# Splits of the second query slab's rotated halves put off by eight steps, first two rounds of attention spread wider

## The chip, the cores and the metric

The kernel runs on one core of a Trainium2 chip, as one program in one launch. The metric is the time of one execution in microseconds (us), as the device gives it. A profiled execution of the kernel before belongs to the numbers; where an engine's busy time, a wait or a line is named, it is from that one execution.

The engines are TensorE (PE in the profile, with PEld for its weight loads), VectorE (DVE), ScalarE (ACT), GpSimd (POOL) and SyncE (SP), whose queue here issues nearly all DMAs.

## What is computed

Two decoder layers over x of 512 x 1024 float32. Cut to what matters:

```python
def hybrid_layer(x, w_in, w_out, g_pre, g_post, lb, g_head, sinks):
    h = rms_norm(x, g_pre)
    q_h, f_h, i_h, z_h, q_a, k_a, v_a, z_a = split(h @ w_in)      # 1024 -> 6400 columns
    o_h = rms_norm(hgrn2(q_h, f_h, i_h, lb), g_head) * silu(z_h)  # 8 heads of 128, gated recurrence
    q_a, k_a = rotary(q_a, pos), rotary(k_a, pos)                 # 16 query heads, 2 key heads of 64
    o_a = sliding_window_attention(q_a, k_a, v_a, sinks) * silu(z_a)   # window 128, blocks of 128
    return x + rms_norm(concat([o_h, o_a]) @ w_out, g_post)
```

The attention takes, for each block of 128 queries, the scores against its own and the previous block of keys, masks them to the window, takes a softmax with one sink term per head, and sums the values.

## The kernel before

**Projections.** The weights come from HBM in pieces of 128 x 512 float32 and are split on the chip into a high half (`whi`, a cast on ScalarE, L176) and a low half (`wlo`, a subtraction on VectorE, L177); activations are split in the same way. A product of two such numbers takes three matmuls, so each step of a projection issues three matmuls of 128 x 512 into a `pj` buffer of PSUM (L282). A unit is eight steps (24 matmuls) that add into one buffer; two units run interleaved. `step()` issues one step, counts down the list `waiting`, and starts the weight conversions that are due at that step count. `later(steps, key, fn)` puts a function on that list: it runs when so many steps have been issued.

**Weight buffers.** Four `raw` buffers take the DMAs on SyncE's queue; nine `whi` and nine `wlo` buffers hold the halves. SyncE issues in order, so a weight load that waits for a free `raw` buffer holds up what stands behind it.

**Queries.** The query projection comes in two slabs of weights (QA and QA + 1) of four units each. Two units make one group g of four heads, so the first slab gives g = 0 and 1, the second g = 2 and 3. `evac` of `qa_stream` is called at the end of each unit. After the first unit of a group it multiplies by cosine and sine on VectorE (L493, L494); after the second it does the same (L499, L500), adds and subtracts on GpSimd (L503, L504), splits the two rotated halves (two casts on ScalarE, L506, and two subtractions on VectorE, L507) and stores them to HBM in two DMAs (L509). `load_q(g)` reads them back in four DMAs in the layout that attention needs (L483).

**Attention.** `att_stream` runs 16 rounds (g, n), g from 0 to 3 and block n from 0 to 3. Round i issues the scores of round i (L531 for n = 0, otherwise two halves, L542), the transposes of the probabilities of round i - 2 (L569) and the value product of round i - 4 (L595). A round's softmax goes through several engines: VectorE masks the scores (L534 or L546), takes the row maxima (L535 or L547) and from them `negm` (L550) and `ds` (L552); ScalarE takes four exponentials out of the score buffer (L556) and that of the sink (L559); VectorE adds and inverts the sums (L560, L561); GpSimd normalises (L563). After the transposes ScalarE and VectorE split the result (L328, L329) and GpSimd masks it twice (L581). Scores and transposes share three PSUM buffers (`sc_78`, `sc_79`, `sc_80`) in turn. The queries of groups 2 and 3 are loaded after rounds 3 and 7, into the two buffers of groups 0 and 1, and first needed in rounds 8 and 12.

**What sets the order.** The attention's rounds and the projections are merged by shares: each stream has a total, and the stream whose share done is the smallest goes next.

```python
def merge(*streams):
    live = [[g, 0.0, float(total)] for g, total in streams]
    while live:
        s = min(live, key=lambda e: e[1] / e[2])
        try:
            s[1] += next(s[0]) or 1.0
```

Each function of a round yields 1 / (functions in that round), so a round counts 1 in a total of 20 (16 rounds and `VLAG` = 4). The program so written is then put in order engine by engine by a scheduler, which moves an instruction ahead of others of its engine if it sees it ready earlier. `pin(ins)` fixes an instruction behind the one written before it on the same engine; the attention's matmuls are pinned, the projection's are not.

Of the kernel before, what the change touches and what calls it, by code (L numbers as in the profile page):

```python
# [11 lines left out]
F32R = mybir.dt.float32r  # L12
U8 = mybir.dt.uint8
AF = mybir.ActivationFunctionType
ALU = mybir.AluOpType
# [5 lines left out]
NT = SEQ // 128  # L21
# [8 lines left out]
QA, IV, FQ, ZA, ZH = 0, 2, 4, 8, 10  # L30
# [4 lines left out]
HG_N = 28.5  # L35
VLAG = 4
QWAIT = 8
DEFER = 18
PJ, SC = 3, 3
LEAD, SPACE = 20, 3  # L40
# [6 lines left out]
# [6 lines that stand above are left out]
        except StopIteration:  # L53
            live.remove(s)
# [13 lines left out]
def hybrid_kernel(ctx: ExitStack, tc: tile.TileContext, x, wkv, win, wout, g_pre, g_post, lbp, ghead, sinks,  # L68
                  gcol_c, cos_f, sin_f, cos_t, sin_t, masks_c, out):
    nc = tc.nc  # L70
# [55 lines left out]
    for l in range(1, DEPTH):  # L126
        i = plan_order.index((l, "kv"))
# [69 lines left out]
    def later(steps, key, fn):  # L197

        waiting.append([steps, key, fn])
# [6 lines left out]
    def ensure(key):  # L206
        while key not in emitted:
            run_first()
# [92 lines left out]
    def through(key):  # L301
        while slab_done[key] < slab_steps[key]:
            step()
            yield 1.0

    def until(cond):
        while not cond():
            step()
# [10 lines left out]
    def proj_feat(key, l, evac):  # L319

        enqueue(key, [(range(KT), lambda k, w, m=m: tuple(t[:, k % 4 * P:(k % 4 + 1) * P] for t in w[2 * m + k // 4]),
                       lambda k, w: (hT[l][0][:, k, :], hT[l][1][:, k, :]), lambda o, m=m: evac(m, o),
                       [("h", l, tt) for tt in range(NT)]) for m in range(4)])
# [33 lines left out]
    class Norm:  # L357
# [47 lines left out]
        def rest(self, c):  # L405
            self.turn(c)
            self.high(c)
            self.low(c)
            if self.tt == NT - 1 and c == 1:
                state["limit"] = None  # L410
# [15 lines left out]
    def layer(l, last):  # L426
# [51 lines left out]
        qs, stacks = {}, {}  # L478

        def load_q(g):  # L480
            st = big.tile([P, 4, 512], F32R, tag="b8", name="qs", bufs=2)
            for row, j, i in ((0, 1, 0), (32, 0, 1), (64, 0, 0), (96, 1, 1)):
                nc.sync.dma_start(st[row:row + 32].bitcast(F32), stacks[g][j, i].rearrange("(h p) t -> p h t", h=4))  # L483
            qs[g] = st

        def qa_stream(s):
            hold = {}

            def evac(m, o):
                cosf, sinf = rot[0][:, 0], rot[0][:, 1]  # L490
                if m % 2 == 0:
                    hold["a"] = a = big.tile([P, 2, 512], F32, tag="oy", name="rot", bufs=6)
                    nc.vector.tensor_tensor(a[:, 0], o, cosf, op=ALU.mult)  # L493
                    nc.vector.tensor_tensor(a[:, 1], o, sinf, op=ALU.mult)  # L494
                    return
                g = 2 * s + m // 2
                a = hold["a"]
                b = big.tile([P, 2, 512], F32, tag="oy", name="rot", bufs=6)
                nc.vector.tensor_tensor(b[:, 0], o, sinf, op=ALU.mult)  # L499
                nc.vector.tensor_tensor(b[:, 1], o, cosf, op=ALU.mult)  # L500
                stack = dr.tile([2, 2, P, 512], F32, tag="stack", name="stack", bufs=4)

                nc.gpsimd.tensor_tensor(a[:, 0], a[:, 0], b[:, 0], op=ALU.subtract)  # L503
                nc.gpsimd.tensor_tensor(b[:, 1], b[:, 1], a[:, 1], op=ALU.add)  # L504
                for r, h in ((a[:, 0], b[:, 0]), (b[:, 1], a[:, 1])):
                    nc.scalar.copy(h.bitcast(F32R), r)  # L506
                    nc.vector.tensor_tensor(r.bitcast(F32R), r, h, op=ALU.subtract)  # L507
                for j, t in ((0, a), (1, b)):
                    nc.sync.dma_start(stack[j].rearrange("i p t -> p i t"), t)  # L509
                stacks[g] = stack  # L510
                if g < 2:
                    load_q(g)

            proj_feat(("in", l, QA + s), l, evac)

# [72 lines left out]
        def att_value(g, n, terms):  # L588
            v = g // 2
            t_ = slice(n * P, (n + 1) * P)  # L590
            if g == len(oa):
                oa.append(big.tile([P, 2, 512], F32, tag="oy", name="oa", bufs=6))
            U = ac()
            for i, (blk, d) in enumerate(terms):
                pin(nc.tensor.matmul(U, lhsT=vst[v][:, blk, :], rhs=d, start=(i == 0), stop=(i == len(terms) - 1)))  # L595
            ul = tmp("u")
            nc.scalar.copy(ul[0:64, :], U[64:128, :])
            Uv = U.rearrange("p (a b t) -> p a b t", a=2, b=2)
            lv = ul.rearrange("p (a b t) -> p a b t", a=2, b=2)
            for b in range(2):  # L600
                nc.vector.tensor_tensor(oa[g][64 * b:64 * b + 64, :, t_], Uv[0:64, :, b, :], lv[0:64, :, b, :], op=ALU.add)

        def att_stream(steps):


            pts, terms = {}, {}
            n = len(steps)
            for tt in range(NT):
                ensure(("k", l, tt))
            for i in range(n + VLAG):  # L610
                todo = []
                if i < n:
                    todo.append(lambda: pts.update({i: att_scores(*steps[i])}))
                if 2 <= i <= n + 1:
                    todo.append(lambda: terms.update({i - 2: att_transpose(*steps[i - 2], pts.pop(i - 2), i % 2)}))
                if i >= VLAG:
                    todo.append(lambda: att_value(*steps[i - VLAG], terms.pop(i - VLAG)))
                for fn in todo:
                    fn()
                    yield 1.0 / len(todo)  # L620

                if i < n and steps[i][1] == NT - 1 and steps[i][0] < 2:
                    until(lambda: steps[i][0] + 2 in stacks)
                    load_q(steps[i][0] + 2)
# [235 lines left out]
        def final(tt, ch, c0, n):  # L860
# [38 lines left out]
            if not last:  # L899
                pre_norm(tt, xt, hT2["gpre"], hT[l + 1], ("h", l + 1, tt), DEFER)  # L900

# [11 lines left out]
        def run():  # L913
            hg = lambda a: (hgrn(a), HG_N)
            rest = lambda key: (through(key), remaining(key))
            until(lambda: 1 in qs)
            for _ in range(QWAIT):
                step()
            merge((att_stream([(g, n) for g in range(4) for n in range(NT)]), 4 * NT + VLAG), rest(("in", l, FQ)))
            merge(hg(0), rest(("in", l, FQ + 1)))  # L920
            merge(hg(2), rest(("in", l, FQ + 2)))
            merge(hg(4), rest(("out", l, "a1")))
            merge(hg(6), rest(("out", l, "h0")))
            kv_room.add(l + 1)
            drain(through(("out", l, "h1")))
# [47 lines left out]
    m, n = head[0], head[1]  # L973
# [146 lines left out]
```

## Time and profile before

| | us |
|---|---|
| median of 3 runs | 934.13 (933.86 to 934.25) |
| the profiled execution | 933.88 |
| its span, first to last instruction | 932.1 |
| around the span | 1.78 |

A profile row of an instruction has its start in us from the start of the span, its duration in us, engine, line, operation, output <- inputs and the count of instructions merged in it; in brackets stands how long its engine was idle before it and whose end released it. Durations of instructions that follow each other on an engine overlap by some hundredths. The granted clock is the share of TensorE's full clock that the throttle let through. The scores of the first attention round start at 58.96 us in layer 0 and at 517.94 us in layer 1.

### The profile page before, as it was taken

What the parts mean: (1) busy time and instruction counts of PE and PEld (TensorE: products, weight loads), DVE (VectorE), ACT (ScalarE), POOL (GpSimd) and SP (SyncE); (2) the same over time, 40 slices, a digit from 0 to 9 for tenths busy, and PEclk for the clock granted to TensorE, in tenths of its full rate; (3) what the DMA queues carried; (4) which work ended last, traced back from release to release, by engine and by line L of the source; (5) the groups of instructions that cost most, each with busy time, mean ns of one, the idle gap of its engine ahead of it and who ended that gap; (6) DMA issues with size and microseconds to landing.
All of it is one profiled execution on the core that took longest, in us unless ns stands there. A gap on an engine that the chain in (4) does not pass through costs nothing.

```text
span 932.1 us, 18970 instructions
## 1 busy us (share of the span) xinstructions
PE 910.0 (98%) x7240; PEld 753.3 (81%) x7240; DVE 670.9 (72%) x1326; ACT 462.8 (50%) x1100; POOL 271.5 (29%) x286
## 2 busy tenths in 40 slices
PE   8998999999999999999989989999999999999996
PEld 7886888878788788788878868888787887887885
DVE  5978777885766783955786788677877577749556
ACT  5535658636464451444453456684554736325242
POOL 3435444232221311311232345441323212113102
PEclk9999999999999999999999989999999999999998
DMA  7685413322222142424356554123223223323313
GB/s 221 193 226 156 124 39 101 91 82 80 68 85 96 62 141 64 138 69 123 111 162 179 171 159 136 35 82 101 70 79 89 71 80 105 111 69 93 91 34 135
DMA packets 56570, 100.74 MB, mean 108 GB/s; under 512 B 6560, under 2 KB 9120, under 8 KB 56480
## 3 DMA queue, kind: packets, MB, share of 16 engines
q1 hardware_dynamic: 56192, 99.40, 35.7%
q8 instruction: 57, 0.93, 0.4%
q14 instruction: 33, 0.27, 0.1%
q10 hardware_dynamic: 288, 0.14, 0.1%
HBM read 86.93 MB, written 12.58 MB: 107 GB/s over the span
## 4 chain that ended last, share of the span: by engine, by line
PE 86%; DVE 6%; ACT 3%; POOL 2%; issue 2%; DMA 1%; SPq 0%; POOLq 0%; DVEq 0%; ACTq 0%
PE pj L282 71%; PE ac L595 2%; PE sc L703 2%; PE sc L542 2%; PE ac L772 2%; ACT s L556 1%; PE ac L775 1%; PE ac L760 1%; PE sc L569 1%; DVE wlo L177 1%; PE sc L820 1%; POOL r L343 1%; PE sc L750 1%; PE sc L714 1%; DVE a L896 1%
## 5 line engine op out<-in xcount | busy, mean ns | idle before, releaser
L282 PE MATMUL pj<-hhi,wlo 128*128 128x512 f32 x512 | 205.8, 402 | 0.0
L177 DVE TENSOR_TENSOR wlo<-raw,whi 128x512 fp32r<-128x512 f32 x249 | 182.9, 748 | 30.0 <-ACT whi L176 28.5
L282 PE MATMUL pj<-hhi,whi 128*128 128x512 f32 x512 | 200.0, 391 | 0.0
L282 PE MATMUL pj<-hlo,whi 128*128 128x512 f32 x512 | 199.5, 390 | 0.0
L176 ACT CAST whi<-raw 128x512 fp32r<-128x512 f32 x256 | 154.5, 621 | 87.9 <-PE pj L282 74.7
L282 PE MATMUL pj<-whi,ops 128*128 128x512 f32 (+1 forms) x520 | 173.5, 395 | 0.0
L282 PEld LDWEIGHTS pj<-whi,ops 128*128 128x128 f32 x520 | 97.2, 188 | 19.6
L282 PEld LDWEIGHTS pj<-hhi,whi 128*128 128x128 f32 x512 | 96.1, 188 | 20.9
L282 PEld LDWEIGHTS pj<-hhi,wlo 128*128 128x128 f32 x512 | 96.2, 188 | 18.7
L282 PEld LDWEIGHTS pj<-hlo,whi 128*128 128x128 f32 x512 | 96.3, 188 | 18.0
L282 PE MATMUL pj<-whi,hlo 128*128 128x512 f32 x256 | 104.5, 408 | 0.7 <-ACT whi L176 0.7
L282 PE MATMUL pj<-wlo,hhi 128*128 128x512 f32 x256 | 101.0, 395 | 2.0 <-DVE wlo L177 2.0
L282 PE MATMUL pj<-whi,hhi 128*128 128x512 f32 x256 | 101.0, 394 | 0.0
L282 PE MATMUL pj<-wlo,ops 128*128 128x512 f32 (+1 forms) x260 | 100.5, 386 | 0.0
L721 POOL TENSOR_TENSOR k<-k,tot 128x256 f32<-128x256 f32 x80 | 64.2, 822 | 109.4 <-PE sc L703 60.7
L556 ACT ACTIVATE s<-sc,negm 128x128 f32<-128x128 f32 x128 | 45.4, 368 | 36.8 <-DVE negm L550 26.1
L720 DVE TENSOR_TENSOR q<-q,tot 128x256 f32<-128x256 f32 x80 | 50.6, 665 | 14.6 <-PE sc L703 9.4
L282 PEld LDWEIGHTS pj<-wlo,hhi 128*128 128x128 f32 x256 | 48.8, 191 | 10.7 <-DVE wlo L177 2.3
L282 PEld LDWEIGHTS pj<-whi,hhi 128*128 128x128 f32 x256 | 48.6, 190 | 10.6
L282 PEld LDWEIGHTS pj<-whi,hlo 128*128 128x128 f32 x256 | 48.6, 190 | 9.6 <-ACT whi L176 1.1
L282 PEld LDWEIGHTS pj<-wlo,ops 128*128 128x128 f32 x260 | 49.0, 188 | 8.7
L563 POOL TENSOR_TENSOR s<-s,sums 128x512 f32<-128x512 f32 x32 | 35.8, 1119 | 57.0 <-ACT a L328 28.4
(185 smaller groups left out, 1418.7 us busy)
## 6 DMA issues: line engine op xcount, KB each, us to landing
raw<-in_win_dram SPq DMA_DIRECT2D x192, 256.0 KB, 2.7
raw<-in_wout_dram SPq DMA_DIRECT2D x64, 256.0 KB, 2.7
stack<-rot SPq DMA_DIRECT2D x16, 512.0 KB, 3.6
qs<-stack SPq DMA_DIRECT2D x32, 256.0 KB, 4.9
a<-in_x_dram SPq DMA_DIRECT2D x12, 256.0 KB, 3.1
raw<-in_wkv_dram SPq DMA_DIRECT2D x8, 256.0 KB, 3.7
x_mid<-a SPq DMA_DIRECT2D x8, 256.0 KB, 2.3
a<-x_mid SPq DMA_DIRECT2D x8, 256.0 KB, 3.0
```

The lines of the kernel that those rows point to most:

```text
L176: keep(nc.scalar.copy(hi, v))
L177: keep((nc.gpsimd if i in on_pool and i % 2 else nc.vector).tensor_tensor(lo, v, hi.bitcast(F32), op=ALU.subtract))
L282: nc.tensor.matmul(u.o, lhsT=u.sta(k, u.w)[i], rhs=u.mov(k, u.w)[j], start=(n == 0), stop=(n == len(u.list) - 1))
L343: keep(nc.gpsimd.tensor_tensor(r, t, mhalf[:, 0:1], op=ALU.pow))
L542: pin(nc.tensor.matmul(S[:, h * 256:(h + 1) * 256], lhsT=q[:, 2 * hp_ + h, t_], rhs=kst[v][p][:, (n - 1) * P:(n + 1) * P], start=(h == 0 a ...
L556: nc.scalar.activation(pt[:, h * P:(h + 1) * P], cur[h], AF.Exp, bias=negm[:, h:h + 1], scale=SCALE, accum_out=sums[:, h:h + 1])
L563: nc.gpsimd.tensor_tensor(pv, pv, sums.unsqueeze(2).broadcast_to([P, 4, P]), op=ALU.mult)
L595: pin(nc.tensor.matmul(U, lhsT=vst[v][:, blk, :], rhs=d, start=(i == 0), stop=(i == len(terms) - 1)))
L703: pin(nc.tensor.matmul(L[32 * b:32 * b + 32, c:c + 16], lhsT=k[:, o_:o_ + 32], rhs=qv[:, blk:blk + qu, 1, :], start=True, stop=True, tile_ ...
L720: nc.vector.tensor_tensor(qv[:, :, 1, :], qv[:, :, 1, :], tv[:, :, 0].unsqueeze(2).broadcast_to([P, nb, hh]), op=ALU.mult)
L721: nc.gpsimd.tensor_tensor(kv_[:, :, 0, :], kv_[:, :, 0, :], tv[:, :, 1].unsqueeze(2).broadcast_to([P, nb, hh]), op=ALU.mult)
L772: pin(nc.tensor.matmul(O[:, c], lhsT=A[:, c], rhs=vs(j, n), start=(n == 0), stop=False))
```

## The change

It has two parts.

The splits of the rotated halves, the stores and the entry in `stacks` move into a function `rest`. For groups 0 and 1 it is called at once, as before. For groups 2 and 3 it goes to `later(ROT_WAIT, ...)`, so it is written out eight projection steps (24 matmuls) later, and its two casts are pinned, behind whatever was last written for ScalarE then. The multiplications and GpSimd's sums stay where they were.

The first two rounds of attention yield 1.75 in place of 1 each, and the total of the stream grows by 1.5: more projection steps are placed in these rounds, and fewer in the later ones.

```diff
+ROT_WAIT = 8
+SLOW = (2, 1.75)
...
-                for r, h in ((a[:, 0], b[:, 0]), (b[:, 1], a[:, 1])):
-                    nc.scalar.copy(h.bitcast(F32R), r)
-                    nc.vector.tensor_tensor(r.bitcast(F32R), r, h, op=ALU.subtract)
-                for j, t in ((0, a), (1, b)):
-                    nc.sync.dma_start(stack[j].rearrange("i p t -> p i t"), t)
-                stacks[g] = stack
+
+                def rest():
+                    for r, h in ((a[:, 0], b[:, 0]), (b[:, 1], a[:, 1])):
+                        keep = pin if g >= 2 else lambda ins: ins
+                        keep(nc.scalar.copy(h.bitcast(F32R), r))
+                        nc.vector.tensor_tensor(r.bitcast(F32R), r, h, op=ALU.subtract)
+                    for j, t in ((0, a), (1, b)):
+                        nc.sync.dma_start(stack[j].rearrange("i p t -> p i t"), t)
+                    stacks[g] = stack
+                    if g < 2:
+                        load_q(g)
+
                 if g < 2:
-                    load_q(g)
+                    rest()
+                else:
+                    later(ROT_WAIT, None, rest)
...
                 for fn in todo:
                     fn()
-                    yield 1.0 / len(todo)
+                    yield (SLOW[1] if i < SLOW[0] else 1.0) / len(todo)
...
-            merge((att_stream([(g, n) for g in range(4) for n in range(NT)]), 4 * NT + VLAG), rest(("in", l, FQ)))
+            merge((att_stream([(g, n) for g in range(4) for n in range(NT)]), 4 * NT + VLAG + SLOW[0] * (SLOW[1] - 1)), rest(("in", l, FQ)))
```

The lines below the change are numbered higher by 2 to 10 in the kernel after: the casts L506 are L511 there, the subtractions L507 are L512, L176 and L177 are L178 and L179, L531 and L542 are L541 and L552, L546 and L547 are L556 and L557, L550 is L560, L556 is L566.

How far the projection has come when the scores of a round are issued, in projection matmuls since the scores of round 0, counted in TensorE's order (where the two halves stand apart, the first):

| round | 1 | 2 | 3 | 4 | 5 | 8 | 12 | 15 |
|---|---|---|---|---|---|---|---|---|
| layer 0, before | 0 | 18 | 36 | 56 | 72 | 123 | 195 | 246 |
| layer 0, now | 12 | 42 | 57 | 84 | 90 | 145 | 204 | 252 |
| layer 1, before | 0 | 20 | 40 | 55 | 67 | 121 | 190 | 241 |
| layer 1, now | 7 | 37 | 52 | 72 | 85 | 140 | 199 | 247 |

TensorE, layer 1, from the scores of round 0 (L531) to those of round 1 (L542), before:

```order
L531 MATMUL sc_80<-kst,qs 128x128 x8
L542 MATMUL sc_78<-kst,qs 128x256 x4
L542 MATMUL sc_79<-kst,qs 128x256 x4
L282 MATMUL pj<-hhi,whi 128x512
L282 MATMUL pj<-hhi,wlo 128x512
```

And now:

```order
L541 MATMUL sc_80<-kst,qs 128x128 x8
L284 MATMUL pj<-hhi,whi 128x512
L284 MATMUL pj<-hhi,wlo 128x512
L284 MATMUL pj<-hlo,whi 128x512
L284 MATMUL pj<-hhi,whi 128x512
L284 MATMUL pj<-hhi,wlo 128x512
L284 MATMUL pj<-hlo,whi 128x512
L284 MATMUL pj<-hhi,whi 128x512
L552 MATMUL sc_78<-kst,qs 128x256 x4
L552 MATMUL sc_79<-kst,qs 128x256 x4
```

Seven projection matmuls have come between the two rounds.

ScalarE, layer 1, around the casts of group 3 before (`rot`; `whi` are weights, `a<-sc` the split of the transposes, `u` a value product):

```order
L559 ACTIVATE es<-ds 128x4
L506 CAST rot<-rot 128x512
L176 CAST whi<-raw 128x512 x2
L506 CAST rot<-rot 128x512
L176 CAST whi<-raw 128x512 x2
L328 CAST a<-sc_78 128x512
L597 COPY u<-ac 64x512
```

The same stretch of ScalarE's queue now, where the casts are those of group 2 and the exponentials (L566) those of round 3:

```order
L330 CAST a<-sc_79 128x512
L178 CAST whi<-raw 128x512
L566 ACTIVATE s,sums<-sc_80,negm 128x128
L178 CAST whi<-raw 128x512
L566 ACTIVATE s,sums<-sc_80,negm 128x128
L178 CAST whi<-raw 128x512
L511 CAST rot<-rot 128x512 x2
L178 CAST whi<-raw 128x512
L566 ACTIVATE s,sums<-sc_78,negm 128x128 x2
L569 ACTIVATE es<-ds 128x4
```

The casts of group 3 no longer stand in front of these weight casts; they come three rounds later. Those of group 2, which stood before the exponentials of round 2, have taken a place behind three weight casts and among the exponentials of round 3.

VectorE, layer 0, around the subtractions of group 3 before (`wlo` are weight low halves, `mx` row maxima, `oa` the attention's output):

```order
L499 TENSOR_TENSOR rot<-pj,cs 128x512
L500 TENSOR_TENSOR rot<-pj,cs 128x512
L177 TENSOR_TENSOR wlo<-raw,whi 128x512
L534 COPY_PREDICATED sc_80<-masks,neg 128x512
L177 TENSOR_TENSOR wlo<-raw,whi 128x512
L507 TENSOR_TENSOR rot<-rot 128x512
L177 TENSOR_TENSOR wlo<-raw,whi 128x512 x2
L507 TENSOR_TENSOR rot<-rot 128x512
L535 TENSOR_REDUCE mx<-sc_80 128x4
L329 TENSOR_TENSOR a<-sc_78,a 128x512
L550 SCALAR_TENSOR_TENSOR negm<-mx,nsnk 128x4
```

And now, with the subtractions of group 2, in round 3:

```order
L556 COPY_PREDICATED sc_80<-masks,sc_80 128x2x128
L556 COPY_PREDICATED sc_78<-masks,sc_78 128x2x128
L557 TENSOR_REDUCE mx<-sc_80 128x2
L179 TENSOR_TENSOR wlo<-raw,whi 128x512
L557 TENSOR_REDUCE mx<-sc_78 128x2
L179 TENSOR_TENSOR wlo<-raw,whi 128x512 x2
L512 TENSOR_TENSOR rot<-rot 128x512 x2
L179 TENSOR_TENSOR wlo<-raw,whi 128x512
L560 SCALAR_TENSOR_TENSOR negm<-mx,nsnk 128x4
L331 TENSOR_TENSOR a<-sc_79,a 128x512
```

Before, two subtractions and four weight low halves stood around the masking and in front of the maxima of round 4; now the same number stands between the maxima of round 3 and its `negm`.

## The prediction

> **What bounds the kernel now.** I read the page first, then the busy time by stretches, then TensorE's instructions in order of time, then the chain of waits and the other engines where TensorE stood. A round is one step of `att_stream`: S(i) are its score matmuls, T(i) its transposes. The three score buffers go round, so S(i+1) and T reuse what the exponentials of earlier rounds must first have read.
>
> ```profile
> span 932.1 us, 18970 instructions
> PE 910.0 (98%) x7240; PEld 753.3 (81%) x7240; DVE 670.9 (72%) x1326; ACT 462.8 (50%) x1100; POOL 271.5 (29%) x286
> PEclk9999999999999999999999989999999999999998
> ```
>
> TensorE is the bound: 910.0 of 932.1 us. Nothing is to be won but where it stands or runs slowly. The change touches the attention rounds alone, 60 to 160 us in layer 0 and 520 to 620 in layer 1. Busy time by stretches (from:to, length; busy time of PE, PEld, DVE, ACT and POOL, each with its instructions; granted clock; DMA share; GB/s):
>
> ```profile
> 60.00:100.00 40.00, 35.98 (x189) 29.61 (x189) 34.99 (x79) 21.60 (x82) 20.07 (x17) 1.00 0.56 151
> 100.00:160.00 60.00, 59.70 (x313) 50.12 (x313) 46.17 (x114) 39.64 (x126) 27.94 (x25) 1.00 0.34 93
> 520.00:580.00 60.00, 55.93 (x275) 45.60 (x274) 52.22 (x113) 36.04 (x125) 28.80 (x25) 0.94 0.50 143
> 540.00:545.00 5.00, 3.12 (x7) 2.51 (x8) 5.00 (x8) 2.73 (x5) 1.28 (x1) 0.62 0.34 116
> 545.00:550.00 5.00, 5.00 (x21) 4.20 (x20) 3.67 (x10) 2.47 (x11) 3.17 (x3) 0.70 1.03 390
> ```
>
> TensorE is idle for 4.02 us (40.00 - 35.98) and 0.30 us in layer 0 and for 4.07 us in layer 1. In layer 1 its clock also falls, to 0.62 and 0.70: 3.12 x 0.38 + 5.00 x 0.30 = 2.69 us. In all 11.08 us can be won. TensorE's longest waits, with what ended them:
>
> ```profile
> 66.31 0.74 PE L542 MATMUL sc<-kst,qs 128*128 128x256 f32 x4 [0.77 <-ACT s L556]
> 72.24 1.44 PE L542 MATMUL sc<-kst,qs 128*128 128x256 f32 x8 [0.61 <-ACT s L556]
> 87.72 0.52 PE L569 MATMUL sc<-ident,s 128*128 128x128 f32 x3 [1.64 <-DVE negm L550]
> 89.24 0.74 PE L542 MATMUL sc<-kst,qs 128*128 128x256 f32 x4 [1.00 <-ACT s L556]
> 539.40 0.50 PE L282 MATMUL pj<-whi,hlo 128*128 128x512 f32 x1 [0.71 <-ACT whi L176]
> 541.88 0.80 PE L282 MATMUL pj<-wlo,hhi 128*128 128x512 f32 x1 [1.99 <-DVE wlo L177]
> 554.30 0.74 PE L542 MATMUL sc<-kst,qs 128*128 128x256 f32 x4 [0.37 <-ACT s L556]
> 579.13 1.44 PE L542 MATMUL sc<-kst,qs 128*128 128x256 f32 x8 [0.23 <-ACT s L556]
> ```
>
> They are of two kinds. At 66.31 and 72.24 the scores of rounds 2 and 3 come before the exponentials of the round before have read the buffer: the rounds stand too close. The larger ones come from the rotated halves of the fourth query group. In layer 0 ScalarE stands 3.94 us at their cast (first row), and the `negm` of the row maxima, queued on VectorE behind the subtractions that wait for the casts, ends only at 87.64:
>
> ```profile
> 82.21 0.62 ACT L506 CAST rot<-rot 128x512 fp32r<-128x512 f32 x1 [3.94 <-POOL rot L503]
> ```
>
> ```profile
> 82.86 1.56 DVE L507 TENSOR_TENSOR rot<-rot 128x512 fp32r<-128x512 f32 x1
> ...
> 85.69 0.68 DVE L507 TENSOR_TENSOR rot<-rot 128x512 fp32r<-128x512 f32 x1
> 86.30 0.68 DVE L535 TENSOR_REDUCE mx<-sc 128x4 f32<-128x512 f32 x1
> 86.90 0.68 DVE L329 TENSOR_TENSOR a<-sc,a 128x512 fp32r<-128x512 f32 x1
> 87.49 0.15 DVE L550 SCALAR_TENSOR_TENSOR negm<-mx,nsnk 128x4 f32<-128x4 f32 x1
> ```
>
> In layer 1 the chain of waits shows the same: GpSimd's rotation, then the cast, then the subtraction. Behind these two stand the weight casts and low halves of which the projection waits for one, the 0.71 and 1.99 above.
>
> ```profile
> 536.89 1.29 POOL rot L503
> 538.18 0.02 issue
> 538.21 0.63 ACT rot L506
> 538.83 0.02 issue
> 538.86 0.04 DVE rot L507
> ```
>
> **The change part by part.** Wider spacing. Before, no projection matmul stands between S(0) and S(1), and 18 (layer 0) or 20 to 24 (layer 1) between S(1) and S(2); now 12 or 7, and then 30. The time of matmuls as they go by without waits, from the chain of waits:
>
> ```profile
> 99.99 0.48 PE sc L542 x4
> 100.47 1.39 PE pj L282 x6
> 101.86 0.43 PE sc L569 x4
> ```
>
> One projection matmul is 1.39 / 6 = 0.23 us, half the scores of a round 0.48 and the transposes 0.43, and 30 matmuls 6.9 us. What they must cover, by durations of single rows:
>
> ```profile
> 62.66 0.75 DVE L547 TENSOR_REDUCE mx<-sc 128x2 f32<-128x256 f32 x2
> 67.78 0.75 DVE L546 COPY_PREDICATED sc<-masks,sc 128x256 f32<-128x256 uint8 x2
> L552 DVE TENSOR_TENSOR ds<-snk,negm x32: 148/162/1253, 62.6 to 615.6; 128x4 f32<-128x4 f32 x32
> 87.68 1.52 ACT s L556 x8
> ```
>
> Masking 0.75, maxima 0.75, `negm` 0.15 and all four exponentials 1.52 make 3.2 us. One of the small steps can last 1253 ns in place of 162, 1.1 us more. So 4.3 us against 6.9: the 0.77 goes. Between S(2) and S(3) 15 matmuls and T(0) cover 15 x 0.23 + 0.43 = 3.9 us; two exponentials are enough there, 0.75 + 0.75 + 0.15 + 0.76 + 1.1 = 3.5 us, since the third group's subtractions (before: in front of those maxima) now stand behind them. The 0.61 goes too.
>
> Putting off the casts. The casts of the third group now stand behind three weight casts on ScalarE, those of the fourth in rounds 6 to 7, when GpSimd's sums are long ready. That ends the 1.64, 1.00, 0.71 and 1.99, and with the pair of 0.71 and 1.99 the fall of the clock that follows it. All 11.08 us go, if nothing comes instead.
>
> What comes instead, first place: layer 0, round 3. The third group's two subtractions and four weight low halves now stand between the maxima of S(3) and its `negm`.
>
> ```profile
> L507 DVE TENSOR_TENSOR rot<-rot x16: 656/814/1564, 41.0 to 542.4; 128x512 fp32r<-128x512 f32 x16
> L177 DVE TENSOR_TENSOR wlo<-raw,whi x249: 626/686/1746, 22.8 to 902.6; 128x512 fp32r<-128x512 f32 x125
> ```
>
> S(4) needs two of S(3)'s exponentials: 0.75 + 0.75 + 4 x 0.69 + 2 x 0.66 + 0.15 + 0.76 = 6.5 us. TensorE has 27 matmuls and T(1) until then: 27 x 0.23 + 0.43 = 6.6. It just fits. But each of the six can be held by a GpSimd instruction (L507's longest is 0.9 over its shortest), and three of those, the fourth group's two rotation sums and one normalisation, fall there. The ends are 0 and 6 x 0.9 - 0.1 = 5.3 us. Of the fourth group's two subtractions above, which met GpSimd's rotation sums, one was held (1.56) and one was not (0.68); I take two of the six, 1.8 - 0.1 = 1.7.
>
> Second place: layer 1, rounds 3 to 5. Here `negm` of S(3) stands ahead of the six, but their casts stand among its exponentials.
>
> ```profile
> 77.10 1.16 ACT L176 CAST whi<-raw 128x512 fp32r<-128x512 f32 x2
> ```
>
> The chain up to S(4)'s exponentials: 1.5 (mask, maxima) + 0.15 + 1.52 + 6 casts x 0.58 + two small steps 0.3 + mask 0.75 + split of T(1) 0.68 + maxima 0.68 + 0.15 + 1.52 = 10.7 us. TensorE has 33 matmuls, T(1), T(2), S(4), two value matmuls and half of S(5) (S(4) counted as two transposes' time, since it has eight matmuls of 128 columns): 7.6 + 0.86 + 0.86 + 0.46 + 0.48 = 10.2. So 0.5 us are missing, and 2.7 with two small steps held for 1.1 each; rows in a queue overlap by some hundredths, so I take 1.2.
>
> Third: the later rounds. The projections are now ahead by 28 matmuls at S(4) in layer 0 (84 against 56) and 17 in layer 1 (72 against 55); from there to S(15) 168 and 175 remain, where there were 190 and 186. These 33 matmuls, 7.6 us, are cover that rounds 5 to 15 lose. They wait for 0.30 + 0.37 + 0.23 = 0.90 us now; I take twice that, with 0.9 and 7.6 as the ends.
>
> At no cost: the weight pieces that are needed sooner. The sixth one's low half was the 1.99; it is now needed 11 (layer 0) or 15 matmuls after S(3), 2.5 us or more, and is the first of the four: 0.75 + 0.75 + 0.15 + 0.69 = 2.3 us after S(3) at the latest. Held once, it would cost 0.7 us. On SyncE's queue the two stores move behind three weight loads and, with the four loads that follow them, have to land before the group's first scores.
>
> ```profile
> stack<-rot SPq DMA_DIRECT2D x16, 512.0 KB, 3.6
> qs<-stack SPq DMA_DIRECT2D x32, 256.0 KB, 4.9
> ```
>
> Their 8.5 us lie under 88 matmuls, 20 us, from S(3) to S(8); without that cover S(8) would wait by what is missing.
>
> The sum: 1.7 + 1.2 + 1.8 = 4.7 us come instead, so 11.1 - 4.7 = 6.4 us are saved. The profiled execution took 933.88 us (span 932.1 and 1.78 around it), 0.25 below the median of 934.13: 927.5, and **927.7** as a median.
>
> **The rivals.** A change of 0.2%, 1.9 us, is about what a measurement here can tell from none; faster is below 932.3 and slower above 936.0.
>
> Nothing comes instead: the six are not held and the later rounds have room (they lost only 0.30 of 60 us). Then all goes: 923.0. Against it: both places fit only to a few tenths.
>
> The clock falls for itself. Then the 2.69 stay: 930.4. The only clock below 1.00 in these rounds follows the pair of 0.71 and 1.99; but in layer 0 the pair of 1.64 and 1.00, as long, was followed by none (1.00 in the row 60:100). The Trainium skill, "TensorE: Matmul & The Clock Gate", section "Why this matters for your kernels", has the clock fall at idle gaps over about 3 us; by that neither pair would do it, and the time would be this rival's. The fall right behind the pair in layer 1 speaks against it.
>
> The cover is given back: all 7.6 us of it turn into waits in rounds 5 to 15. 1.7 + 1.2 + 7.6 = 10.5, 0.6 saved: 933.5, no change. For it speaks that VectorE is busy for 52.22 of 60 us; against it that the weights' low halves come by projection steps, so earlier too, and leave rounds 8 to 15 lighter.
>
> Slower: the six subtractions are held by GpSimd. With three or more held round 3 of layer 0 waits as long (3 x 0.9 - 0.1 = 2.6 us) as the pair that the fall of the clock followed, and would lose 2.7 more; in layer 1 the upper end, 2.7, does the same. At four held it becomes slower: 3.5 + 2.7 + 2.7 + 2.7 + 1.8 = 13.4 us come instead of 11.1, 936.4; at six 15.2, 938.2. I take 937.3, between them. Against it: GpSimd has three instructions there for six subtractions.
>
> **How the numbers follow.** The forecast has 0.52 and runs from 924.4 (0 + 0.5 + 0.9 come instead) to 931.3 (the first place at its end, 3.6 more). Nothing comes instead: 0.12. The clock for itself: 0.08. Cover given back: 0.16. Slower: 0.12. The range from 923.0 to 933.5 holds the first three and half of the fourth, some 0.80. Faster: 0.52 + 0.12 + 0.08 and a little of the fourth, 0.74; same: the rest of it, 0.14; slower 0.12.
>
> **What would show it.** Right: no wait of TensorE over 0.5 us at S(2) and S(3), no wait of ScalarE at the casts of the rotated halves, the granted clock at 1.00 in all rounds, and about 4 to 5 us idle in place of 8.4, the largest at S(4) of layer 0 behind `negm`. Wrong: a clock below 1.00 behind round 3; waits in rounds 8 to 12 of over 2 us in all; a projection matmul that waits for a weight's low half for over 0.5 us.

## The result and the profile after

The kernel after takes **927.7 us** (median of 4 runs, 927.27 to 928.83); in the same series the kernel before takes 934.0. The ratio is 0.9938, 95% interval 0.9925 to 0.9952. Repeated in a later series it was 0.9943 (0.9928 to 0.9957, median 928.15). The prediction was 927.7.

The page of the profiled execution (927.92 us, span 926.2):

```profile
span 926.2 us, 18985 instructions
PE 908.4 (98%) x7240; PEld 751.1 (81%) x7240; DVE 672.1 (73%) x1326; ACT 462.5 (50%) x1100; POOL 268.8 (29%) x286
PEclk9999999999999999999999999999999999999999
```

No slice of the clock is below 9 any more. The same stretches as before, busy time of the five engines, granted clock, DMA share and GB/s:

```profile
60.00:100.00 40.00, 39.87 (x211) 33.42 (x211) 31.74 (x79) 22.11 (x84) 18.86 (x17) 1.00 0.51 134
100.00:160.00 60.00, 58.80 (x303) 48.12 (x303) 50.19 (x113) 40.94 (x128) 26.31 (x24) 1.00 0.39 105
520.00:580.00 60.00, 58.73 (x304) 48.38 (x303) 50.56 (x121) 38.48 (x137) 29.06 (x26) 1.00 0.47 139
580.00:620.00 40.00, 39.15 (x202) 32.23 (x201) 32.32 (x72) 28.52 (x82) 17.97 (x16) 1.00 0.20 60
```

TensorE is idle for 0.13 + 1.20 + 1.27 + 0.85 = 3.45 us in the rounds where it was for 8.39, and the 2.69 us of slow clock are gone: 7.63 us less. What is left, the longest waits of TensorE, with two score groups that have no wait in brackets:

```profile
112.73 0.74 PE L552 MATMUL sc<-kst,qs 128*128 128x256 f32 x4 [0.19 <-ACT s L566]
117.66 1.40 PE L552 MATMUL sc<-kst,qs 128*128 128x256 f32 x8
142.79 1.44 PE L552 MATMUL sc<-kst,qs 128*128 128x256 f32 x8 [0.79 <-ACT s L566]
149.07 1.44 PE L552 MATMUL sc<-kst,qs 128*128 128x256 f32 x8
...
535.90 0.50 PE L284 MATMUL pj<-wlo,hhi 128*128 128x512 f32 x1 [0.17 <-DVE wlo L179]
543.87 0.75 PE L552 MATMUL sc<-kst,qs 128*128 128x256 f32 x4 [0.60 <-ACT s L566]
569.29 0.74 PE L552 MATMUL sc<-kst,qs 128*128 128x256 f32 x4 [0.31 <-ACT s L566]
599.35 1.44 PE L552 MATMUL sc<-kst,qs 128*128 128x256 f32 x8 [0.79 <-ACT s L566]
```

The waits lie at S(9), S(14) and, in layer 1, S(5). The row at 149.07, S(15), shows a cost that no bracket names: its eight score matmuls last 1.44 us, before 1.12 (in layer 1 1.44 and 1.11). S(10), at 117.66, lasts 1.40 without a bracket; before it lasted 1.44 behind a wait of 0.30. From the scores of round 0 to the first matmul of the recurrence the rounds became 2.27 us shorter in layer 0 (129.63 to 127.36) and 3.98 in layer 1 (131.12 to 127.14). That is about 0.7 in each less than idle time and clock give (2.99 and 4.64): for the same matmuls TensorE is busy longer, in layer 0 for 126.03 us in place of 125.31. S(15) is a part of it; where the rest lies, these rows do not show. Layer 0 also starts 0.31 later.

The casts of the rotated halves on ScalarE, and VectorE in round 3 of layer 0, the place for which the prediction had taken its largest cost:

```profile
76.76 1.16 ACT L511 CAST rot<-rot 128x512 fp32r<-128x512 f32 x2
99.96 1.14 ACT L511 CAST rot<-rot 128x512 fp32r<-128x512 f32 x2
...
78.97 2.04 DVE L179 TENSOR_TENSOR wlo<-raw,whi 128x512 fp32r<-128x512 f32 x2
80.94 1.28 DVE L512 TENSOR_TENSOR rot<-rot 128x512 fp32r<-128x512 f32 x2
82.75 0.15 DVE L560 SCALAR_TENSOR_TENSOR negm<-mx,nsnk 128x4 f32<-128x4 f32 x1
```

The casts wait for nothing, in layer 1 neither. In round 3 only the pair of weight low halves at 78.97 is held (2.04 for two of 0.69), the subtractions are not, `negm` ends at 82.90, and S(4) at 83.85 waits for nothing.

### The profile page after: what moved, and what is told of

It reads as the page before. It is cut to its first block, busy times and chain, and to the rows that moved or that the text cites. A ratio compares the mean times of both kernels' runs of the same rounds, so it can differ in the third digit from the quotient of the medians.

```text
span 926.2 us, 18985 instructions
## 1 busy us (share of the span) xinstructions
PE 908.4 (98%) x7240; PEld 751.1 (81%) x7240; DVE 672.1 (73%) x1326; ACT 462.5 (50%) x1100; POOL 268.8 (29%) x286
## 4 chain that ended last, share of the span: by engine, by line
PE 85%; DVE 8%; ACT 3%; issue 2%; POOL 1%; DMA 0%; POOLq 0%; DVEq 0%; SPq 0%; ACTq 0%
PE pj L284 71%; PE sc L713 2%; PE sc L552 2%; PE ac L605 2%; DVE wlo L179 2%; PE ac L782 2%; PE ac L785 1%; PE ac L770 1%; ACT s L566 1%; PE sc L579 1%; PE sc L830 1%; DVE mx L557 1%; POOL r L345 1%; DVE a L331 1%; PE sc L760 1%
## 5 line engine op out<-in xcount | busy, mean ns | idle before, releaser
L179 DVE TENSOR_TENSOR wlo<-raw,whi 128x512 fp32r<-128x512 f32 x249 | 182.5, 746 | 27.1 <-ACT whi L178 26.2
L178 ACT CAST whi<-raw 128x512 fp32r<-128x512 f32 x256 | 155.0, 621 | 84.1 <-PE pj L284 71.5
L566 ACT ACTIVATE s<-sc,negm 128x128 f32<-128x128 f32 x128 | 45.5, 368 | 38.6 <-DVE negm L560 38.6
L681 DVE RECIPROCAL a<-f 128x256 f32<-128x256 f32 x16 | 28.0, 1750 | 28.4 <-ACT f L658 26.1
```

Of the source, the lines that this page charges most:

```text
L178: keep(nc.scalar.copy(hi, v))
L179: keep((nc.gpsimd if i in on_pool and i % 2 else nc.vector).tensor_tensor(lo, v, hi.bitcast(F32), op=ALU.subtract))
L566: nc.scalar.activation(pt[:, h * P:(h + 1) * P], cur[h], AF.Exp, bias=negm[:, h:h + 1], scale=SCALE, accum_out=sums[:, h:h + 1])
L681: nc.vector.reciprocal(re, f2[:, :, 1])
```

## The experiments

All are short edits of the kernel after, except the one that says so. "Same chip" is the kernel before on the chip of that run.

| run | us (median) | same chip | ratio (95%) |
|---|---|---|---|
| after, repeated | 928.15 | 934.05 | 0.9943 (0.9928 to 0.9957) |
| putting off and pin alone | 935.55 | 933.42 | 1.0031 (1.0019 to 1.0044) |
| spacing alone | 928.22 | 933.42 | 0.9955 (0.9942 to 0.9967) |
| after without the pin | 929.78 | 933.42 | 0.9971 (0.9959 to 0.9982) |
| pin alone | 935.12 | 933.42 | 1.0015 (1.0006 to 1.0025) |
| putting off and pin, no sums of the fourth group | 930.31 | 934.05 | 0.9961 (0.9947 to 0.9976) |
| before, attention 8 steps later | 935.00 | 934.05 | 1.0017 (1.0007 to 1.0027) |
| putting off and pin, attention 8 steps later | 933.43 | 934.11 | 0.9999 (0.9991 to 1.0008) |
| spacing of 2.5 | 933.35 | 934.05 | 0.9997 (0.9987 to 1.0006) |
| put off by 4 steps | 929.12 | 933.69 | 0.9951 (0.9935 to 0.9967) |
| put off by 16 steps | 933.06 | 933.69 | 0.9994 (0.9985 to 1.0003) |
| spacing of 1.95, round 13 of 1.2 | 927.17 | 933.69 | 0.9930 (0.9915 to 0.9944) |

### Each part alone

Putting off and pin alone:

```diff
-SLOW = (2, 1.75)
+SLOW = (2, 1.0)
```

> Putting off and pinning alone; the first two rounds spaced as before. My theory (two parts that end separate waits): the waits of S(2) and S(3) in layer 0 come back (0.77 and 0.61, 1.4 us), those at the casts do not, the clock stays at 1.00, and rounds 5 to 15 have the cover back that the spacing took, so that the 0.79 at S(14) of both layers goes or shrinks: 927.7 + 1.4 - 0.8 = 928.3 us, between 927.5 and 929.5. Rival, the spacing does it all: about 934. Rival, the spacing buys nothing (what it ends early comes back late): 927.0 to 927.7.

It is slower than before, by 0.3%. My theory falls here: putting off does not end the waits of layer 0, it exchanges them for one that is longer, and adds two more at S(9). Of the two waits that the prediction gave to the spacing, the 0.77 at S(2) is back, but the 0.61 at S(3) is not. TensorE's waits of this kernel:

```profile
87.80 1.22 PE L552 MATMUL sc<-kst,qs 128*128 128x256 f32 x4 [3.40 <-DVE oa L611]
115.19 0.74 PE L552 MATMUL sc<-kst,qs 128*128 128x256 f32 x4 [1.75 <-ACT s L566]
...
542.53 0.51 PE L284 MATMUL pj<-wlo,hhi 128*128 128x512 f32 x1 [1.01 <-DVE wlo L179]
573.05 0.75 PE L552 MATMUL sc<-kst,qs 128*128 128x256 f32 x4 [1.77 <-ACT s L566]
```

The releaser named in the first row is only the one that the profile saw last. The score buffers tell more. In TensorE's order the second half of S(5) goes into the buffer of S(4) (projection matmuls left out):

```
L541 MATMUL sc_80<-kst,qs 128x128 x8
...
L579 MATMUL sc_78<-ident,s 128x128 x4
...
L552 MATMUL sc_79<-kst,qs 128x256 x4
...
L552 MATMUL sc_80<-kst,qs 128x256 x4
```

So S(4)'s mask, maxima, `negm` and exponentials have to be through before it. VectorE and GpSimd between these two:

```profile
80.00 0.74 DVE L544 COPY_PREDICATED_SCALAR sc<-masks,neg 128x512 f32 x1
80.66 4.28 DVE L179 TENSOR_TENSOR wlo<-raw,whi 128x512 fp32r<-128x512 f32 x3
84.86 0.68 DVE L545 TENSOR_REDUCE mx<-sc 128x4 f32<-128x512 f32 x1
86.06 0.14 DVE L560 SCALAR_TENSOR_TENSOR negm<-mx,nsnk 128x4 f32<-128x4 f32 x1
...
79.50 1.74 POOL L505 TENSOR_TENSOR rot<-rot 128x512 f32<-128x512 f32 x1
81.21 1.73 POOL L506 TENSOR_TENSOR rot<-rot 128x512 f32<-128x512 f32 x1
82.91 1.48 POOL L573 TENSOR_TENSOR s<-s,sums 128x512 f32<-128x512 f32 x1
```

Three weight low halves stand between mask and maxima, and they take 1.43 us each on average in place of 0.69, while GpSimd adds the halves of the fourth group and then normalises. They stood there before too; VectorE of the kernel before in the same place, and the second of GpSimd's sums:

```profile
80.94 0.74 DVE L534 COPY_PREDICATED_SCALAR sc<-masks,neg 128x512 f32 x1
81.60 1.12 DVE L177 TENSOR_TENSOR wlo<-raw,whi 128x512 fp32r<-128x512 f32 x1
...
84.35 1.43 DVE L177 TENSOR_TENSOR wlo<-raw,whi 128x512 fp32r<-128x512 f32 x2
...
82.13 1.74 POOL L504 TENSOR_TENSOR rot<-rot 128x512 f32<-128x512 f32 x1
```

With the two subtractions between them (1.56 and 0.68) the five took from 81.60 to 86.37, 4.77 us; the three alone now take 4.28. Before, one low half (1.12) and one subtraction (1.56) ran beside GpSimd's sums, which ended at 83.87, and the other three ran behind them, at about 0.7 each; now all three low halves run beside GpSimd. S(5)'s second half starts 10.33 us behind S(4) (77.47 to 87.80), before 10.66 (78.58 to 89.24): almost nothing is gained. In the kernel after it is 4.90 (83.85 to 88.75), with 12 projection matmuls, 2.8 us, in between, where there are 19 here and were 22 before.

Spacing alone:

```diff
-keep = pin if g >= 2 else lambda ins: ins
+keep = lambda ins: ins
...
-if g < 2:
-    rest()
-else:
-    later(ROT_WAIT, None, rest)
+rest()
```

> Wider spacing alone; the splits of all groups written at once and without the pin. My theory: 0.77 and 0.61 of layer 0 go, the waits behind the casts of the rotated halves stay (2.6 us in layer 0, 2.7 and the fall of the clock, 2.7, in layer 1), and rounds 5 to 15 wait for some 1 to 2 us more: 934.0 - 1.4 + 1.5 = 934 us, between 932.5 and 935.5. Rival, the spacing does it all (with more room between the rounds the casts are no longer late): 927.7. Rival, the clock falls for itself, whatever the waits: its fall would show in a kernel without the waits too.

The rival holds for the larger part: 0.9955, some 4.2 of the 5.3 to 5.8 us. The parts do not add up: -4.2 and +2.9 alone make -1.3, together they make -5.3 or more. What spacing alone leaves is the other kind of wait, weight casts behind the casts of the rotated halves. ScalarE and TensorE in layer 1:

```profile
533.36 0.62 ACT L511 CAST rot<-rot 128x512 fp32r<-128x512 f32 x1 [1.74 <-POOL rot L505]
536.04 0.62 ACT L511 CAST rot<-rot 128x512 fp32r<-128x512 f32 x1 [2.07 <-POOL rot L506]
536.57 2.18 ACT L178 CAST whi<-raw 128x512 fp32r<-128x512 f32 x4
...
537.24 0.73 PE L284 MATMUL pj<-whi,hlo 128*128 128x512 f32 x2 [1.67 <-ACT whi L178]
```

The clock falls behind it (clock is the third number from the end):

```profile
535.00:540.00 5.00, 3.33 (x14) 2.20 (x13) 3.85 (x9) 2.70 (x5) 1.01 (x1) 0.87 0.14 13
540.00:545.00 5.00, 5.00 (x25) 4.27 (x25) 2.51 (x7) 2.81 (x12) 3.15 (x3) 0.79 1.02 364
```

The kernel after has 0.17 in that place. What putting off adds to the spacing in time is small. By the ratios, 0.9955 against 0.9943 and 0.9938, it would be 1.1 to 1.6 us, but the intervals overlap. The five executions of spacing alone took 927.82, 928.07, 928.22, 929.45 and 929.61 us; the profiled one, with the fall, is that of 929.45, and the fall cost it 1.48 us (worked out below). The mean granted clock was 0.998 or 0.999 in the first three and 0.996 and 0.997 in the last two. That the first three went without the fall is likely, but of them there is no trace. They are as short as those of the kernel after, repeated (927.63 to 928.80): beyond the end of that fall, a gain from putting off on top of the spacing is not shown.

Without the pin:

```diff
-keep = pin if g >= 2 else lambda ins: ins
+keep = lambda ins: ins
```

> The change without the pin: the casts of groups 2 and 3 are written eight steps later, but the scheduler may move them, and its order puts those of the fourth group back ahead of weight casts, those of the third ahead of the first exponential. My theory: what counts is where the casts stand in ScalarE's queue, so most of the waits behind them come back: between 930 and 934 us, with a wait of ScalarE of over 2 us at a cast of rotated halves. Rival, writing them later is enough: 927.7, with no such wait.

As expected in part: 929.78, just under the range given. The casts wait again (1.87 and 1.11 in layer 0, 1.87 and 1.63 in layer 1), though none for over 2 us, and S(5) waits for 1.78 and 1.07. Spacing alone, in the same series, took 928.22: writing the splits later wins nothing unless they are fixed there. (The profiled execution took 931.42, 1.64 over the median.)

The pin alone:

```diff
-SLOW = (2, 1.75)
+SLOW = (2, 1.0)
...
-if g < 2:
-    rest()
-else:
-    later(ROT_WAIT, None, rest)
+rest()
```

> The pin alone: the splits are written at once, as before, and only fixed where they are written; the spacing as before. My theory: ScalarE then stands at the casts until GpSimd's sums are done, as before or longer (over 3.5 us), and the late maxima and weight halves stay: 934 to 937 us. Rival, the pin is all that counts: 928 to 929.

As expected, 935.12: the casts wait for 2.31 and 1.07 in layer 0, in all nearly the 3.5 expected, and `negm` makes the transposes wait for 2.36. The profile is of the shortest of eleven executions, 932.82. Seven took 935.10 to 935.81, at a mean granted clock of 0.993 or 0.994 in place of its 0.996; what they waited for beyond this, no trace shows.

### Does GpSimd hold VectorE?

The kernel with putting off and pin alone once more, without the two sums of the fourth group, whose queries so stay unrotated:

```diff
-nc.gpsimd.tensor_tensor(a[:, 0], a[:, 0], b[:, 0], op=ALU.subtract)
-nc.gpsimd.tensor_tensor(b[:, 1], b[:, 1], a[:, 1], op=ALU.add)
+if g < 3:
+    nc.gpsimd.tensor_tensor(a[:, 0], a[:, 0], b[:, 0], op=ALU.subtract)
+    nc.gpsimd.tensor_tensor(b[:, 1], b[:, 1], a[:, 1], op=ALU.add)
```

> Putting off and pinning alone (as in the first of these runs), without GpSimd's two sums of the fourth query group (L505 and L506 for g = 3), in both layers: the fourth group's queries are left unrotated. Every engine's other instructions stand in the same order. The new theory (what costs is VectorE's queue between masking and negm of the round in which GpSimd sums the fourth group, since each operation there is held): the three weight low halves take 2.0 us in place of 4.28, the wait of 3.40 at S(5) of layer 0 falls to about 1.1 and the clock stays at 1.00: 935.55 - 2.3 - 1.0 = 932.2 us, between 931 and 933. Rival, the low halves are late for another reason (their casts, their loads) and GpSimd holds nothing: 935.5, with the wait of 3.40 as it was.

```profile
80.58 1.47 POOL L574 TENSOR_TENSOR s<-s,sums 128x512 f32<-128x512 f32 x1
...
81.74 2.07 DVE L179 TENSOR_TENSOR wlo<-raw,whi 128x512 fp32r<-128x512 f32 x3
...
86.67 0.73 PE L553 MATMUL sc<-kst,qs 128*128 128x256 f32 x4 [1.23 <-ACT s L567]
```

The same three low halves take 2.07, the 3.40 becomes 1.23, and in layer 1 the 1.01 goes and the 0.89 becomes 0.17. The span is 3.7 us shorter (932.5 to 928.8); the time, 930.31, is a little better than expected, though the clock did not stay at 1.00: it fell behind the wait at S(9), which stays (1.76, with the sums 1.75). So the hold by GpSimd is shown. It is not that of the sums alone, for without them the normalisation, too, comes earlier (80.58 in place of 82.91) and is nearly over when the low halves start. The Trainium skill, "SBUF — State Buffer", section "Who interferes with whom", has VectorE operations with two inputs in SBUF contend with a GpSimd instruction that reads SBUF. The rows agree: 1.43 on average beside GpSimd's work, 0.69 without it.

### Is it enough that the projection runs ahead?

With the spacing the last of the fourth group's products comes behind S(3) (76.36 against 75.59), before behind S(4) (78.93 against 78.58). I took it that only the round counts, and moved the group in another way, in the kernel before:

```diff
-QWAIT = 8
+QWAIT = 16
```

> The kernel before, with attention started eight projection steps (24 matmuls) later (QWAIT 16 in place of 8); splits at once, no pin, no spacing. The scores of rounds 1 to 4 then stand 18, 33, 51 and 78 matmuls behind those of round 0, and the products of the fourth group between S(2) and S(3), not behind S(4). The new theory (what counts is in which round the fourth group falls): the waits at T(3) and S(5) of layer 0 (1.64 and 1.00) and the 1.99 of layer 1 go, and with 18 matmuls between S(0) and S(1) most of the 0.77: 927 to 930 us. Rival, what counts is the room of 30 matmuls between S(1) and S(2): 932 to 934.

This theory falls too: 935.0. S(5) is cured (0.78 for 1.64 + 1.00), but the weight casts stand behind the rotated halves again, and S(8) is new:

```profile
81.19 0.73 PE L282 MATMUL pj<-whi,hlo 128*128 128x512 f32 x2 [1.66 <-ACT whi L176]
110.08 1.11 PE L531 MATMUL sc<-kst,qs 128*128 128x128 f32 x8 [1.68 <-ACT s L556]
...
541.45 0.73 PE L282 MATMUL pj<-whi,hlo 128*128 128x512 f32 x2 [1.42 <-ACT whi L176]
```

Then the same start with putting off and pin, in the kernel after:

```diff
-QWAIT = 8
+QWAIT = 16
...
-SLOW = (2, 1.75)
+SLOW = (2, 1.0)
```

> Putting off and pinning together with attention started eight steps later (QWAIT 16 in place of 8), without the wider spacing: S(1) to S(4) stand 18, 33, 51 and 72 matmuls behind S(0). In VectorE's order the subtractions of the third group stand in round 2, those of the fourth in round 7, and none in rounds 4 and 8. The theory (the spacing helps by letting the projection run ahead, so that the fourth group is through by round 3, and the putting off then keeps the weight casts from waiting behind GpSimd's sums; either alone leaves one of the two): no wait of over 1 us in rounds 2 to 8, 927.5 to 929.5 us. Rival, the room of 30 matmuls between S(1) and S(2) itself is needed: waits of 0.5 to 1 us at S(2) and S(3) in both layers, 930 to 932 us.

Layer 0 went by the theory: no wait over 0.32 in rounds 2 to 8, and 2.04 us idle from 60 to 160. Layer 1 went by the rival:

```profile
518.65 3.17 DVE L179 TENSOR_TENSOR wlo<-raw,whi 128x512 fp32r<-128x512 f32 x2
...
530.04 0.74 PE L552 MATMUL sc<-kst,qs 128*128 128x256 f32 x4 [1.97 <-ACT s L566]
548.81 0.74 PE L552 MATMUL sc<-kst,qs 128*128 128x256 f32 x4 [1.08 <-ACT s L566]
```

The third group's sums now meet the first round: two weight low halves are held (3.17 for two) ahead of its mask. The exponentials of the first round come late by that, a weight cast stands among them, and VectorE waits 1.84 us for it in the midst of S(1)'s masking; 15 matmuls between S(1) and S(2) do not cover that. In the kernel after no weight low half runs beside these sums in layer 1, and 30 matmuls stand between S(1) and S(2). So the spacing gives two things, the lead and another place for the third group's sums, with more room; whether layer 1 needs the place or the room, this run does not separate. The whole time, 933.43, is 4 us over what I expected, of which the waits of layer 1 over after's (4.32 against 1.27 idle from 520 to 580) are 3.

### How much of each

Spacing of 2.5:

```diff
-SLOW = (2, 1.75)
+SLOW = (2, 2.5)
```

> The change with the first two rounds spaced by 2.5 in place of 1.75: S(2) stands 60 matmuls behind S(0), S(3) 73 and S(4) 79. The new theory: the fourth group falls ahead of S(2), which was good already; now S(4) follows S(3) after 6 matmuls (1.4 us), which covers no exponentials, so a wait of 1 to 3 us comes in round 3 or 4, and the later rounds have lost more: 928.5 to 931 us. Rival, more room in the first rounds is better still: below 927.

Worse than expected, 933.35. The pinned casts now fall right behind S(4) (85.57 against 84.95 in layer 0), their subtractions there ahead of its mask (2.11 for two), and S(5) waits for 1.10 and 2.04, behind which the clock falls to 0.68. S(7) of layer 0 waits for 0.56, S(9) for 1.00 and 0.98, S(14) for 0.87 twice. In all TensorE stands 8.53 us in the rounds, about as long as in the kernel before (8.39).

Put off by four steps:

```diff
-ROT_WAIT = 8
+ROT_WAIT = 4
```

> The change with the splits put off by four steps in place of eight; the spacing as in the change. In VectorE's order the fourth group's two subtractions then stand in round 4, ahead of the masking of S(4) in layer 0 and between the masking and the maxima of S(4) in layer 1; in the change they stand in round 7. The theory after the runs so far (the extra work on VectorE costs where it stands in front of the maxima of S(4) or S(8), whose next round comes after only 5 to 6 us, and nothing in rounds 3 and 7): two subtractions of 0.7 to 1.5 us each add 1 to 2 us to the wait at S(5) in each layer: 930 to 932 us. Rival, putting off as such is what counts, by how much does not: 928.

The mechanism shows in layer 0, the two subtractions beside a normalisation on GpSimd ahead of S(4)'s mask:

```profile
85.55 2.10 DVE L512 TENSOR_TENSOR rot<-rot 128x512 fp32r<-128x512 f32 x2
...
91.69 0.73 PE L552 MATMUL sc<-kst,qs 128*128 128x256 f32 x4 [1.77 <-ACT s L566]
```

In layer 1 nothing was added (0.68 at S(5), after 0.60), and the waits at S(9) are gone since the subtractions have left round 7. At 929.12 it is just under the expected range; by the time alone it cannot be told from the kernel after (0.9951 against 0.9943 and 0.9938, the intervals overlap), and so not the theory from its rival.

And by sixteen:

```diff
-ROT_WAIT = 8
+ROT_WAIT = 16
```

> The change with the splits put off by sixteen steps. In VectorE's order the third group's subtractions stand ahead of the masking of S(3), together with the fourth group's products and a weight low half, and the fourth group's in round 5. The same theory: round 3 has 27 to 29 matmuls of room and costs under 1 us, round 5, with 16 matmuls (3.7 us) to S(6), costs about 1 us in each layer: 929 to 931 us. Rival, later is as good or better: 928 or less.

A miss, 933.06. The waits are not those of the theory: the third group's subtractions stand ahead of weight low halves, for which the projection waits 1.21 (layer 0) and 1.36 (layer 1), and smaller ones follow at S(5), S(7) and S(8).

Spacing of 1.95, and 1.2 for round 13:

```diff
-SLOW = (2, 1.75)
+SLOW = (2, 1.95)
+LATE = (13, 1.2)
...
-yield (SLOW[1] if i < SLOW[0] else 1.0) / len(todo)
+yield (SLOW[1] if i < SLOW[0] else LATE[1] if i == LATE[0] else 1.0) / len(todo)
```

The total of the stream grows with it.

> The change with the first two rounds spaced by 1.95 and round 13 by 1.2. In VectorE's order no subtraction of the rotated halves stands in rounds 4, 5 and 8 any more, the third group's stand in round 2, the fourth group's in round 7; 21 matmuls stand between S(13) and S(14) in place of 18 (layer 1: as many). The same theory: the waits of 0.79 at S(14) go in both layers and those of about 0.6 at S(5) shrink, so 1.5 to 2.5 us less than the change: about 926 us. Rival, room given to one round is taken from another and comes back as a wait there: 928.

Both 0.79 at S(14) are gone, S(5) of layer 1 is 0.46 in place of 0.60. S(9) takes most of it back, 1.25 in layer 0 and 0.96 in layer 1, where it was 0.19 and 0.31, as the rival had it. The expected 926 is missed: 927.17. At 0.9930 it is 0.1% under after, within both intervals: not shown to be better.

The changed kernel itself, repeated:

> The changed kernel once more, on the chip of the runs below, as the measure for them. Both theories: 0.994 of the kernel before, as measured (0.9925 to 0.9952).

As expected. Its profile has 4.22 us idle in the rounds and the clock at 1.00, with one wait that the first profile did not have, 0.68 at S(5) of layer 0.

## Why the prediction was right, and where it was not

The time was right, and the idle time was near (3.45 and 4.22 us in the two profiles, 4.7 predicted). How the gain was assigned to the two parts was wrong, and so was where the largest wait would be: not at S(4) of layer 0, which waits for nothing, but at S(14).

- **Spacing ends 0.77 and 0.61**: right for the 0.77; the 0.61 is gone without the spacing too (putting off and pin alone). But the spacing does far more: alone it is worth 4.2 us, where the prediction gave it 1.4.
- **"Putting off the casts ... ends the 1.64, 1.00, 0.71 and 1.99"**: this step failed as a cause. Alone it makes the kernel slower (1.0031). I took the late `negm` for a matter of the casts that wait for GpSimd. The rows of the kernel before spoke against it: between 81.60 and 87.49 VectorE stood idle for only about 0.14 us, so it hardly waited for the casts. The runs show another cause in the same place: weight low halves and subtractions in VectorE's queue between S(4)'s mask and `negm` are held while GpSimd sums the fourth group and normalises, and when the subtractions leave, the weight low halves beside them are held instead. With the spacing, where the sums come a round earlier, that goes; then putting off ends what is left, the weight casts behind the rotated halves.
- **The clock**: right, 1.00 in all rounds in both profiles.
- **First place, layer 0 round 3, 1.7 us**: mis-sized, 0 there (in the repeat 0.68 at S(5)). One pair of the weight low halves was held, the third group's subtractions were not. The share of two in six rested on a misreading: of the two subtractions before, the one that was not held (85.69) did not meet GpSimd's sums, which had ended at 83.87.
- **Second place, layer 1 rounds 3 to 5, 1.2 us**: 0.17 + 0.60 = 0.77; the `negm` of S(4) was itself held there, 0.55 us at 541.67 in place of 0.15.
- **Later rounds, 1.8 us**: 1.20 in layer 0, and 0.16 + 0.31 + 0.79 = 1.26 in layer 1, 2.5 in all; the largest, 0.79, at S(14) of both layers, which the prediction did not name in its sum.
- **The sum**: 3.45 us idle came in place of 4.7. That the time still fits is in part luck: 7.6 us of waits and slow clock went, not 6.4, but 0.7 in each layer came back as matmuls that take longer without a bracket, and 0.31 in the start, neither of which the prediction had.

**The rivals.** "Nothing comes instead" is out by the 3.45 and the 1.7 beside it. "The clock falls for itself" is out: with the waits gone it did not fall in either profile. "The cover is given back" is out at 2.5 of 7.6 us. At a spacing of 2.5 the whole gain is given back, but how much of that is lost cover and how much the subtractions ahead of S(4)'s mask, no run separates. "Slower" had the right mechanism, VectorE held by GpSimd behind a mask; it needed the fourth group in round 4, and the spacing had moved it away.

## What to carry to other kernels

An edit that moves work out of an engine's queue has to be judged by what else stands in that place, above all where another engine holds whatever runs there. Two parts that end the same waits do not add up: run each alone before a gain is given to one of them. And a total that fits says little of its terms; only the runs with one part told here which of them carried it. Where the executions of one kernel scatter by 2 us, a single profile shows only one of them.

## What the runs showed of the hardware

**The clock falls behind waits much shorter than 3 us, but not behind all.** With spacing alone it fell behind one wait of 1.67 us (above). Without the pin, behind 1.78 at 89.90 in layer 0:

```profile
85.00:90.00 5.00, 3.22 (x17) 2.57 (x15) 3.61 (x8) 2.12 (x11) 3.19 (x4) 1.00 1.07 270
90.00:95.00 5.00, 5.00 (x19) 4.14 (x20) 3.26 (x11) 2.37 (x11) 2.37 (x3) 0.66 0.21 38
```

In the kernel without the fourth group's sums it fell behind 1.76 at 112.60 of layer 0:

```profile
110.00:115.00 5.00, 3.24 (x16) 2.63 (x15) 5.00 (x10) 3.42 (x12) 3.05 (x2) 0.88 0.73 242
115.00:120.00 5.00, 5.00 (x20) 4.10 (x19) 4.65 (x12) 3.10 (x11) 2.65 (x3) 0.78 1.07 225
```

In the profiled executions it did not fall behind 1.77 (put off by 4 steps), 1.97 (putting off and pin, attention later) or 2.31 (pin alone, layer 1), nor in the kernel without the sums behind the 1.77 at the same place of layer 1, 569.23. The Trainium skill, "TensorE: Matmul & The Clock Gate", section "Why this matters for your kernels", warns of gaps over about 3 us; with putting off alone the clock did fall behind 3.40, to 0.77, but the falls behind 1.67 to 1.78 show that shorter ones can do it. Each cost 1.5 to 1.7 us here (3.33 x 0.13 + 5.00 x 0.21 = 1.48; 5.00 x 0.34 = 1.70), about as much again as the wait. What decides between two waits of like length stays open; no profile whose longest wait in the rounds was under 1.4 us showed a fall there.

Nor need one kernel behave alike each time. In one series of 23 executions the kernel before took 931.88 to 932.38 us nine times, at a mean granted clock of 0.996 or 0.997, and 933.50 to 935.22 fourteen times, at 0.992 to 0.995; the profiled execution, with the fall of 2.69 us, had 933.88 and 0.994. That the nine went without the fall is likely, not shown: they left no trace.
